# A two-layer trunk on one core: seven products of quarters for eight in layer 0's second FFN product too, three row tiles at the head of both FFNs, and the second half of the tokens completed first

## The chip, the cores and the metric

The kernel runs on one core of a Trainium2 chip. The metric is the device time of one execution in microseconds (us), lower is better. PE is the matrix engine TensorE, DVE is VectorE, ACT is ScalarE, POOL is GpSimd, and SP is the engine whose queue issues nearly all DMAs here.

## The reference

The kernel computes two transformer-like layers in float32 on 512 tokens of width 1024. Layer 0 has a gated-MLP mixer, layer 1 an attention whose keys, values and forget gates are projected once, after layer 0 (the "kv stage"). Both layers end with a SwiGLU FFN of hidden width 2816. Every sublayer is normalised before and after, with shift, scale and gate that come from a conditioning vector `c`:

```
for layer in range(2):
    mod = c_act @ ada_w[layer] + ada_b[layer]
    sh_m, sc_m, g_m, sh_f, sc_f, g_f = split(mod, 6)
    ...
    h = modulate(rms_norm(x, pre_ffn_g[layer]), sh_f, sc_f)
    g, u = split(h @ ffn_w_gu[layer], 2)
    y = (silu(g) * u) @ ffn_w_down[layer]
    x = x + g_f * rms_norm(y, post_ffn_g[layer])
    if layer == 0:
        k, v, dcum = shared_kv(x, c_act @ kv_ada_w + kv_ada_b, ...)
```

## The kernel before, in words

**Products.** Each float32 operand is split into a rounded part "hi" and a remainder "lo" (`load_split`, L112, for loaded weights), and each product is three matmuls: hi by hi, hi by lo, lo by hi. A matmul of 128x512 is the usual piece. Tokens are 4 tiles of 128; the hidden width of the FFN is 22 row tiles of 128. Weights stream from DRAM through a ring of three tiles of 512 KB called `raw` (L110).

**FFN, first product** (`ffn`, L483). For row tile m the gate half and the up half (each 512 KB of `w_gu`, 24 matmuls of 128x512, L504) are formed, then `act` (L506) computes SiLU and the product. The first two row tiles are done in halves of 256 tokens, so that PE can work on tokens 0 to 255 while the hidden state of tokens 256 to 511 is still being normalised, transposed on PE (L277) and split (`prenorm_half`, L268). The lo part of row tile 1's weights is computed on POOL, its hi part on DVE (L525). The normalisation itself is a string of small DVE and ACT steps (`rsqrt1`, L158) that ends in the scaled row `xr` on ACT (L265), on which the transposes wait.

**FFN, second product.** Layer 0 uses `moving` (L284): two column halves, 11 weight pieces each, 3x2 matmuls for each of 4 token tiles, 528 matmuls of 128x512 in all. Layer 1 (`fast`) uses `down` (L362): tokens and columns are halved, the hidden pieces too, and 7 products of quarters (accumulated in X, Z, Y, W and V) replace 8, 462 matmuls (L397 to L399). Its operands are sums of quarters: those of the activations are formed on POOL during the first product (`sums`, L519), those of the weights on DVE (`weight_sums`, L468), which loads `w_down` (two times 512 KB for each pair of row tiles), makes four subtractions of 128x512 and writes four sums to DRAM (`td`), to be loaded again in `down`.

**Background blocks.** The adaLN vectors of later stages come from 512 KB blocks of `ada_w` and `kv_ada_w`: each is loaded to an SBUF tile and reduced against `c` by one DVE instruction (`ada_block`, L181 to L184). They wait in a list `bg`, and `run_bg` emits one or two at given points: 64 of them belong to layer 0's FFN. While a pool is on the stack `bgp` the block is loaded into a tile `rawb` with a single buffer, else into the `raw` ring:

```
raw = bgp[-1].tile([P, 1024], F32, name="rawb", bufs=1) if bgp else raw_tile()
nc.sync.dma_start(raw, src)
nc.vector.tensor_tensor_reduce(raw, raw, c_bc, 1.0, 0.0, mul, add, dst)
```

A `rawb` load can be issued only when the reduce before it has ended, and SP issues its DMAs in the order in which they stand, as DVE executes its instructions.

**What sets the order.** The tile framework's scheduler orders each engine's instructions from the program text, its priorities (`high_priority` in `boundary`) and its own estimates; the order is fixed when the program is built. At the end of layer 0's FFN, `done` (in `boundary`) adds the residual and, for each pair of token tiles, normalises, transposes and splits the hidden state of the kv stage (`evac_h`, L245), whose V and forget-gate products follow for token tiles (0, 1) and then (2, 3) (L859).

Of the kernel before, what the change touches and what calls it, by code (L numbers as in the profile page):

```python
# [68 lines left out]
def tile_yoco_trunk(ctx: ExitStack, tc: tile.TileContext, x, c, cols, ada_t, kv_ada_t,  # L69
# [42 lines left out]
    def load_split(src, width=1024, lo_eng=nc.vector, pool=None, bufs=2, slot=1024, hi_eng=None):  # L112
# [3 lines left out]
        hi = pool.tile([P, slot], F32R, name="whi", tag="whi", bufs=bufs)  # L116
# [4 lines left out]
        lo = pool.tile([P, slot], F32R, name="wlo", tag="wlo", bufs=bufs)  # L121
# [240 lines left out]
    def down(src, td, qa, qb, fp, fw, row, done):  # L362
# [7 lines left out]
        ss = fw.tile([P, 2 * NT], F32, name="ss", bufs=1)  # L370
        X, Z = ([acc.tile([P, 512], F32, name="acc") for _ in range(2)] for _ in range(2))
        Y, W = ([aux.tile([P, 512], F32, name="ps_x", tag=t) for _ in range(2)] for t in ("ps_t", "ps_s"))

# [11 lines left out]
        def parts_q(q, n, held):  # L385

            if held:
                hi, lo = (fp.tile([P, 1024], F32R, name="qh", tag="qb", bufs=NP)[:, :n * H] for _ in range(2))
            else:
                hi, lo = (wp.tile([P, 1024], F32R, name=t, tag=t, bufs=2)[:, :n * H] for t in ("whi", "wlo"))  # L390
            ACT(hi, q, AF.Copy)
            TT(lo, q, f32(hi), sub)
            return lambda i, t: tuple(x[:, i * H + t * P:i * H + t * P + P] for x in (hi, lo))
# [7 lines left out]
        def half_piece(i):  # L401
            r0 = raw_tile()
            nc.sync.dma_start(r0[:, :512], src[0, i, :, 512:])
            return r0[:, :512]

        def held_tile(name, dt=F32):
            return fp.tile([P, 2, 512], dt, name=name, tag="qa", bufs=NP)

        for i in range(NP):
            r0, r1 = raw_tile(), raw_tile()  # L410
            nc.sync.dma_start(r0[:, :512], src[0, i, :, :512])
            nc.sync.dma_start(r0[:, 512:], td[i][:, 0])
            nc.sync.dma_start(r1.rearrange("p (a c) -> p a c", a=2), td[i][:, 1:3])
            a = parts_q(qa[i].rearrange("p q c -> p (q c)"), 4, False)
            for z, (w, bank) in enumerate(((r0[:, :512], X), (r0[:, 512:], Z), (r1[:, :512], Y), (r1[:, 512:], W))):
                w = parts(w)
                for t in range(2):
                    prod(bank[t], a((3, 1, 2, 0)[z], t), w, i == 0, i == NP - 1)
        u2 = held_tile("u2")
        uw = [held_tile("uw") for _ in range(2)]  # L420
        for t in range(2):
            nc.scalar.copy(u2[:, t], X[t])
        for t in range(2):
            TT(u2[:, t], Y[t], u2[:, t], add)
        for t in range(2):
            TT(uw[t][:, 1], Z[t], u2[:, t], add)
            TT(uw[t][:, 0], W[t], u2[:, t], add)
        V = [aux.tile([P, 512], F32, name="ps_x", tag="ps_t") for _ in range(2)]
        held = []
        for i in range(NP):  # L430
            last = i >= NP - TAIL
            r1 = raw_tile()
            nc.sync.dma_start(r1[:, :512], td[i][:, 3])
            nc.sync.dma_start(r1[:, 512:], src[1, i, :, 512:])
            a = parts_q(qb[i].rearrange("p q c -> p (q c)")[:, H:], 3, last)
            b22 = parts(r1[:, 512:], held=last)
            if last:
                held.append([i, a, b22, parts(r1[:, :512])])
                continue
            b21, w3 = parts(half_piece(i)), parts(r1[:, :512])  # L440
# [887 lines left out]
```

## Time and profile before

| | before |
|---|---|
| median of 3 runs | 1385.38 us (1384.28, 1385.38, 1388.41) |
| the profiled execution | 1390.92 us |
| its span, first to last instruction | 1389.2 us |
| PE, DVE, ACT, POOL busy | 96%, 65%, 41%, 20% of the span |
| mean granted clock of PE | 0.989 |
| mean DMA rate | 159 GB/s |

The profiled execution is 5.5 us above the median. Times in the rows count from the start of its span. A row of a timeline gives start, duration, engine, line, operation, tiles and, in brackets, how long the engine had been idle and what released it.

### The profile page before, as it was taken

The page shows a single profiled execution, that of the slowest core. Times are in us where ns is not written, and L with a number is a line of the kernel's source. Part 1 is how long each engine was busy: PE and PEld are TensorE (multiplying, and loading weights), DVE is VectorE, ACT ScalarE, POOL GpSimd, SP SyncE. Part 2 cuts the span into 40 slices and gives each one's busy share as a digit, 9 for nine tenths or more (in the row PEclk, how much of TensorE's full clock was granted, in tenths as well). Part 3 has the DMA queues.
Part 4 walks back from the last instruction along what each step waited for, and adds up shares of the span by engine and source line. Part 5 has one row for each costly group of instructions (what it writes and reads, how often), then busy time and mean ns, then how long its engine had stood idle before and what let it go on. Part 6 is the DMA issues. An engine that isn't in the chain of part 4 may idle for free.

```text
span 1389.2 us, 17713 instructions
## 1 busy us (share of the span) xinstructions
PE 1339.1 (96%) x6463; PEld 1113.0 (80%) x6463; DVE 903.0 (65%) x1569; ACT 572.2 (41%) x983; POOL 278.8 (20%) x228
## 2 busy tenths in 40 slices
PE   6999999998999999899999999999989999999997
PEld 4788888778888888787899777888778888888875
DVE  7888957667545555553554867888676544546777
ACT  5233442354223232123553436778542222224664
POOL 4700000013111111000110535563041211212000
PEclk9999999999999999999999999999999999999999
DMA  8565436833666666673233231011327757565654
GB/s 325 167 218 157 136 110 197 281 110 108 213 201 204 188 193 205 214 249 119 68 104 92 85 96 47 31 32 32 106 77 242 241 177 256 188 213 174 191 152 159
DMA packets 69497, 220.84 MB, mean 159 GB/s; under 512 B 8353, under 2 KB 8609, under 8 KB 69410
## 3 DMA queue, kind: packets, MB, share of 16 engines
q1 hardware_dynamic: 68834, 218.66, 49.4%
q8 instruction: 51, 0.84, 0.3%
q10 hardware_dynamic: 576, 1.05, 0.2%
q14 instruction: 36, 0.29, 0.1%
HBM read 206.03 MB, written 13.65 MB: 158 GB/s over the span
## 4 chain that ended last, share of the span: by engine, by line
PE 57%; DVE 8%; DMA 7%; ACT 2%; issue 2%; POOL 0%; DVEq 0%; SPq 0%; ACTq 0%; POOLq 0%
PE acc L504 32%; PE acc L1012 3%; DMA rawb<-in_ada_t 3%; PE acc L301 3%; PE acc L302 3%; PE acc L300 3%; DMA raw<-in_w_down 2%; DMA raw<-in_ada_t 2%; PE acc L1100 1%; DVE wlo L122 1%; PE ps_z L1053 1%; PE ps_x L277 1%; PE acc L1080 1%; PE ps_s L1065 1%; PE acc L1232 1%
## 5 line engine op out<-in xcount | busy, mean ns | idle before, releaser
L504 PE MATMUL acc<-hT,whi 128*128 128x512 f32 (+1 forms) x1536 | 428.8, 372 | 0.0
L118 ACT ACTIVATE whi<-raw 128x1024 fp32r<-128x1024 f32 (+2 forms) x178 | 185.1, 1041 | 449.1 <-PE acc L504 190.0
L504 PEld LDWEIGHTS acc<-hT,whi 128*128 128x128 f32 x1536 | 273.3, 189 | 49.8
L122 DVE TENSOR_TENSOR wlo<-raw,whi 128x1024 fp32r<-128x1024 f32 (+2 forms) x178 | 218.7, 1230 | 143.3 <-ACT whi L118 141.7
L504 PE MATMUL acc<-hT,wlo 128*128 128x512 f32 (+1 forms) x768 | 267.7, 373 | 0.0
L504 PEld LDWEIGHTS acc<-hT,wlo 128*128 128x128 f32 x768 | 137.3, 190 | 25.0
L184 DVE CUSTOM_DVE_ANT_0 rawb<-rawb,c_bc 128x1024 f32<-128x1024 f32 x62 | 79.0, 1274 | 102.2 <-DMA rawb<-in_ada_t 69.3
L301 PE MATMUL acc<-wlo,hT 128*128 128x512 f32 (+1 forms) x352 | 135.8, 386 | 4.4 <-DVE wlo L122 4.3
L302 PE MATMUL acc<-whi,hT 128*128 128x512 f32 (+1 forms) x352 | 135.4, 385 | 0.0
L300 PE MATMUL acc<-whi,hT 128*128 128x512 f32 (+1 forms) x352 | 135.2, 386 | 0.0
L259 POOL TENSOR_TENSOR hT<-hfull,hT 128x256 fp32r<-128x256 f32 (+1 forms) x43 | 44.0, 1033 | 251.1 <-DVE hT L258 126.1
L301 PEld LDWEIGHTS acc<-wlo,hT 128*128 128x128 f32 x352 | 66.5, 189 | 18.7 <-DVE wlo L122 6.3
L300 PEld LDWEIGHTS acc<-whi,hT 128*128 128x128 f32 x352 | 66.4, 189 | 12.8
L302 PEld LDWEIGHTS acc<-whi,hT 128*128 128x128 f32 x352 | 66.5, 189 | 12.5
L517 POOL TENSOR_TENSOR hid<-sg,hid 128x512 fp32r<-128x512 f32 (+1 forms) x24 | 35.8, 1493 | 198.8 <-ACT hid L516 198.8
L122 POOL TENSOR_TENSOR wlo<-raw,whi 128x1024 fp32r<-128x1024 f32 x20 | 54.9, 2751 | 78.6 <-DVE whi L120 46.9
L301 PE MATMUL acc<-wlo,hid 128*128 128x512 f32 x144 | 56.7, 393 | 3.5 <-DVE wlo L122 3.5
L382 DVE TENSOR_TENSOR hT<-raw,hT 128x512 fp32r<-128x512 f32 x69 | 46.3, 703 | 18.3 <-ACT hT L381 18.2
L300 PE MATMUL acc<-whi,hid 128*128 128x512 f32 x144 | 56.2, 391 | 1.3 <-ACT junk L327 1.1
L184 DVE CUSTOM_DVE_ANT_0 raw<-raw,c_bc 128x1024 f32<-128x1024 f32 x34 | 42.9, 1261 | 22.2 <-DMA raw<-in_ada_t 22.2
L302 PE MATMUL acc<-whi,hid 128*128 128x512 f32 x144 | 56.2, 390 | 0.0
L381 ACT ACTIVATE hT<-raw 128x512 fp32r<-128x512 f32 x69 | 41.7, 627 | 26.1 <-DMA raw<-in_w_down 7.7
(336 smaller groups left out, 2480.9 us busy)
## 6 DMA issues: line engine op xcount, KB each, us to landing
raw<-in_w_gu SPq DMA_DIRECT2D x88, 512.0 KB, 4.4
raw<-in_ada_t SPq DMA_DIRECT2D x50, 512.0 KB, 4.6
rawb<-in_ada_t SPq DMA_DIRECT2D x46, 512.0 KB, 4.2
raw<-in_w_down SPq DMA_DIRECT2D x44, 512.0 KB, 4.3
raw<-in_w_in SPq DMA_DIRECT2D x32, 512.0 KB, 3.7
raw<-in_w_down SPq DMA_DIRECT2D x33, 256.0 KB, 3.0
raw<-in_w_out SPq DMA_DIRECT2D x16, 512.0 KB, 3.7
rawb<-in_kv_ada_t SPq DMA_DIRECT2D x16, 512.0 KB, 3.7
```

The lines of the kernel that those rows point to most:

```text
L118: ACT(hi[:, :width], raw[:, :width], AF.Copy)
L122: lo_eng.tensor_tensor(lo[:, :width], raw[:, :width], f32(hi[:, :width]), sub)
L184: nc.vector.tensor_tensor_reduce(raw, raw, c_bc, 1.0, 0.0, mul, add, dst)
L259: last = lo_eng.tensor_tensor(lo, full, f32(hi), sub)
L300: MM(banks[n], lh, wh, start=kt == 0, stop=False)
L301: MM(banks[n], lh, wl, start=False, stop=False)
L302: MM(banks[n], ll, wh, start=False, stop=kt == kts - 1)
L381: ACT(hi, w, AF.Copy)
L382: TT(lo, w, f32(hi), sub)
L504: MM(o, (hi, hi, lo)[z][:, ks], h[z == 1][kt][:, cs], start=i == 0, stop=i == 3 * KT - 1)
L517: nc.gpsimd.tensor_tensor(hid[1][m][:, cs], sg, f32(hid[0][m][:, cs]), sub)
L1012: pin(MM(box[0], (hi, hi, lo)[z][:, cs], h[z == 1][kt], start=kt + z == 0, stop=kt == KT - 1 and z == 2))
```

## The change

It has four parts.

1. **`down` for both layers.** `ffn` loses its parameter `fast` and the plain path. Layer 0's first product now also holds `weight_sums` and `sums`; its second product is `down`.
2. **Head.** `FIRST = 3` row tiles are done in halves of 256 tokens, and all their weights are split on ACT and DVE, none on POOL. The third tile's parts lie in slots of the pool that later hold `qb`.
3. **`down` in another order.** After the loop that fills X, Z, Y and W, V is completed for all pieces, and token tiles 2 and 3 are finished (`second`) before the last Z and X products, which finish token tiles 0 and 1. Background blocks are emitted in the first loop (`run_bg(1)`) and use `rawb` in the pool `fd`.
4. **kv stage.** The V and forget-gate products take token tiles (2, 3) first.

```diff
-    def down(src, td, qa, qb, fp, fw, row, done):
+    def down(src, td, qa, qb, fp, fd, row, done):
...
         for i in range(NP):
...
+            r0 = halves(src[0, i, :, :512], td[i][:, 0])
+            r1 = halves(td[i][:, 1], td[i][:, 2])
+            a = parts_q(qa[i])
+            run_bg(1)
+            for z, (w, bank) in enumerate(zip(r0 + r1, (X, Z, Y, W))):
                 w = parts(w)
                 for t in range(2):
                     prod(bank[t], a((3, 1, 2, 0)[z], t), w, i == 0, i == NP - 1)
...
-        for i in range(NP):
-            last = i >= NP - TAIL
...
-            for t in range(2):
-                prod(Z[t], a(1, t), b22, False, False)
-            for t in range(2):
-                prod(X[t], a(2, t), b21, False, False)
-            for t in range(2):
-                prod(V[t], a(0, t), w3, i == 0, False)
...
+        for i in range(0, NP, 2):
+            two = range(i, min(i + 2, NP))
+            r, a = halves(*(td[k][:, 3] for k in two)), parts_q(*(qb[k][:, 1:2] for k in two))
+            for k in two:
+                w = parts(r[k - i])
+                for t in range(2):
+                    prod(V[t], a(k - i, t), w, k == 0, k == NP - 1)
         g = row()
...
+        second(0)
+        held = []
+        for i in range(2, NP):
...
+        second(1)
         for t in range(2):
...
-    def ffn(layer, h, row, done, fast=False):
+    def ffn(layer, h, row, done):
...
-                    if fast:
-                        i = m // 2
-                        outs = ((qb[i][:, 3], qa[i][:, 0]) if m % 2 else (qa[i][:, 3], qb[i][:, 0]))
-                        for z, half in enumerate(range(cs.start // H, cs.stop // H)):
-                            TT(outs[half], sg[:, z * H:z * H + H], u[:, z * H:z * H + H], mul)
-                        return
-                    TT(sg, sg, u, mul)
-                    ACT(hid[0][m][:, cs], sg, AF.Copy)
-                    nc.gpsimd.tensor_tensor(hid[1][m][:, cs], sg, f32(hid[0][m][:, cs]), sub)
+                    i = m // 2
+                    outs = ((qb[i][:, 3], qa[i][:, 0]) if m % 2 else (qa[i][:, 3], qb[i][:, 0]))
+                    for z, half in enumerate(range(cs.start // H, cs.stop // H)):
+                        TT(outs[half], sg[:, z * H:z * H + H], u[:, z * H:z * H + H], mul)
...
-                ws = [[load_split(w_gu[layer, m, j], pool=(wp, fw)[m], hi_eng=(None, nc.vector)[m],
-                                  lo_eng=(nc.vector, nc.gpsimd)[m]) for j in range(2)] for m in range(2)]
+                ws = [[load_split(w_gu[layer, m, j], pool=(wp, fw, fp)[m], tag=(None, None, "qb")[m],
+                                  bufs=(2, 2, NF // 2)[m]) for j in range(2)] for m in range(FIRST)]
...
-                for m in range(2, NF):
+                for m in range(FIRST, NF):
...
-                        if m > 2:
+                        if m > FIRST:
                             with behind_norm():
                                 run_bg(1 if layer else 1 + j)
...
-                    if fast and m % 2:
+                    if m % 2:
                         sums(m // 2)
                         weight_sums(w_down[layer], m // 2, td[m // 2])
...
-                moving([w_down[layer, 0, i] for i in range(NF // 2)], NF, 512, lhs, first_half(y0, ss, row))
-                moving([w_down[layer, 1, i] for i in range(NF // 2)], NF, 512, lhs,
-                       lambda n, ps: done(n, ps, y0, ss, row()), tail=6,
-                       tail_load=lambda i, src: load_split_h(src) if i > 1 else cols_of(load_split(src), 512))
+                bgp.append(fd)
+                down(w_down[layer], td, qa, qb, fp, fd, row, done)
+                bgp.pop()
...
-            for grp in ((0, 1), (2, 3)):
+            for grp in ((2, 3), (0, 1)):
```

**PE at the head of layer 0's FFN**, from the last half row before the first transposes of tokens 256 to 511 to the last ones (`xr` is the scaled row of a token tile, `hT` the hidden state, `whi` and `wlo` the parts of a weight tile). Before:

```order
L504 MATMUL acc<-hT,whi 128x256 x16
L277 MATMUL ps_x<-ident,xr 128x128 x4
L504 MATMUL acc<-hT,wlo 128x256 x8
L504 MATMUL acc<-hT,whi 128x256 x16
L504 MATMUL acc<-hT,wlo 128x256 x8
L504 MATMUL acc<-hT,whi 128x256 x9
L277 MATMUL ps_x<-ident,xr 128x128 x12
```

Now:

```order
L531 MATMUL acc<-hT,whi 128x256 x16
L278 MATMUL ps_x<-ident,xr 128x128 x4
L531 MATMUL acc<-hT,wlo 128x256 x8
L531 MATMUL acc<-hT,whi 128x256 x16
L531 MATMUL acc<-hT,wlo 128x256 x8
L531 MATMUL acc<-hT,whi 128x256 x16
L531 MATMUL acc<-hT,wlo 128x256 x8
L531 MATMUL acc<-hT,whi 128x256 x13
L278 MATMUL ps_x<-ident,xr 128x128 x12
```

Between the two groups of transposes stood 41 matmuls of 128x256; now 69 stand there. The same rows stand at the head of layer 1's FFN.

**SP in layer 0's second product** (`rawb` is the single background buffer; `td4` to `td10` hold the stored weight sums; numbers behind a name tell tiles apart). Before, in the first column half:

```order
L183 DMA raw_4564<-in_ada_t 128x1024
L183 DMA rawb_4253<-in_ada_t 128x1024
L114 DMA raw_4591<-in_w_down 128x1024
L183 DMA raw_4597<-in_ada_t 128x1024
L183 DMA rawb_4256<-in_ada_t 128x1024
L114 DMA raw_4624<-in_w_down 128x1024
L183 DMA raw_4630<-in_ada_t 128x1024
L183 DMA rawb_4295<-in_ada_t 128x1024
```

Now, where V is formed:

```order
L184 DMA rawb_4639<-in_ada_t 128x1024
L382 DMA raw_5312<-td4_2619 128x512
L382 DMA raw_5312<-td5_2620 128x512
L382 DMA raw_5341<-td6_2621 128x512
L382 DMA raw_5341<-td7_2622 128x512
L184 DMA rawb_4692<-in_ada_t 128x1024
L184 DMA rawb_4745<-in_ada_t 128x1024
L382 DMA raw_5370<-td8_2623 128x512
L382 DMA raw_5370<-td9_2624 128x512
L382 DMA raw_5399<-td10_2625 128x512
L184 DMA rawb_4798<-in_ada_t 128x1024
```

Two loads of 256 KB now share one tile of the ring, background loads stand between the loads of one tile and the next, and two of them follow each other directly. Of the 64 background loads of this FFN, 50 stand ahead of the last loads of the first loop of `down` and 14 from there to the first loads of the kv weights `w_vf`; before, the last stood in the first column half.

**DVE at the end of layer 0's second product** (L184, now L185, is the reduce of a background block; the CASTs into `hT` make the hi parts of the kv stage's hidden state). Before, the last two reduces:

```order
L184 ISA rawb_4405,A_f1_2608<-rawb_4405,c_bc_75 128x1024
L184 ISA A_f1_2608 128x1
L122 TENSOR_TENSOR wlo_4760<-raw_4756,whi_4758 128x1024
L184 ISA rawb_4408,A_f1_2608<-rawb_4408,c_bc_75 128x1024
L184 ISA A_f1_2608 128x1
L205 TENSOR_TENSOR A_f1_2608<-A_f1_2608,colv_78 128x8
L206 SCALAR_TENSOR_TENSOR A_f1_2608<-A_f1_2608,colv_78 128x8
L122 TENSOR_TENSOR wlo_4805<-raw_4801,whi_4803 128x1024
L331 TENSOR_TENSOR y0_4420<-acc_4431,grow_3191 128x512
```

Now, the last reduce:

```order
L185 ISA rawb_5418,B_f1_2609<-rawb_5418,c_bc_75 128x1024
L185 ISA B_f1_2609 128x1
L165 SCALAR_TENSOR_TENSOR rq_0_5828<-sx2_2611 128x1
L259 CAST hT_5698<-hfull_5730 128x256
L255 TENSOR_SCALAR hfull_5744<-ps_x_5739,A_kv_2603,B_kv_2604 128x256
L168 RECIPROCAL rst2_2610<-rq_1_5829 128x1
L259 CAST hT_5699<-hfull_5734 128x256
L169 TENSOR_TENSOR rq_1_5829<-rst2_2610 128x1
L255 TENSOR_SCALAR hfull_5748<-ps_x_5739,A_kv_2603,B_kv_2604 128x256
```

The last reduce stood ahead of the column half that was still to come; now it stands directly ahead of the first hidden state of the kv stage.

## Rows read from the trace of the kernel before

**Rows 1.** Page, part 1: PE's busy time, share of the span, instructions.
```profile
PE 1339.1 (96%) x6463; PEld 1113.0 (80%) x6463; DVE 903.0 (65%) x1569; ACT 572.2 (41%) x983; POOL 278.8 (20%) x228
```

**Rows 2.** Windows by stage: us, busy (x) of PE, PEld, DVE, ACT, POOL; PEclk, DMA, GB/s.
```profile
330.00:540.00 210.00, 210.00 (x991) 176.66 (x991) 111.41 (x153) 65.66 (x85) 35.74 (x27) 1.00 0.63 193
...
540.00:640.00 100.00, 95.12 (x414) 76.97 (x413) 56.31 (x80) 21.41 (x28) 4.13 (x3) 1.00 0.67 212
...
1037.00:1274.00 237.00, 237.00 (x1106) 199.25 (x1105) 124.51 (x167) 63.21 (x77) 51.27 (x48) 0.99 0.64 209
...
1274.00:1389.00 115.00, 104.43 (x455) 84.70 (x453) 86.56 (x137) 67.06 (x113) 2.24 (x2) 0.98 0.55 172
```

**Rows 3.** PE timeline, layer 0, head of FFN: start, us, instruction, [idle before <-releaser].
```profile
305.05 1.53 PE L277 MATMUL ps_x<-ident,xr 128*128 128x128 f32 x12 [0.31 <-ACT xr L265]
...
317.25 0.66 PE L277 MATMUL ps_x<-ident,xr 128*128 128x128 f32 x4 [1.54 <-ACT xr L265]
...
326.91 2.82 PE L277 MATMUL ps_x<-ident,xr 128*128 128x128 f32 x12 [4.09 <-ACT xr L265]
```

**Rows 4.** PE timeline, layer 1, head of FFN.
```profile
1034.45 2.82 PE L277 MATMUL ps_x<-ident,xr 128*128 128x128 f32 x12 [4.10 <-ACT xr L265]
...
1042.06 1.12 PE L504 MATMUL acc<-hT,wlo 128*128 128x256 f32 x8
1043.02 2.08 PE L504 MATMUL acc<-hT,whi 128*128 128x256 f32 x16
```

**Rows 5.** DVE timeline, layer 0, same head as rows 3.
```profile
320.63 2.35 DVE L164 SCALAR_TENSOR_TENSOR rq<-sx 128x1 f32<-128x1 f32 x1
...
323.45 1.83 DVE L168 TENSOR_TENSOR rq<-rst 128x1 f32<-128x1 f32 x1
325.32 0.16 DVE L169 SCALAR_TENSOR_TENSOR rq<-rq,rq 128x1 f32<-128x1 f32 x1
```

**Rows 6.** POOL timeline, layer 0, same head as rows 3.
```profile
320.19 5.07 POOL L122 TENSOR_TENSOR wlo<-raw,whi 128x1024 fp32r<-128x1024 f32 x2 [5.55 <-DVE whi L120]
```

**Rows 7.** PE timeline, layer 0, second FFN product, to the first kv matmul (L867).
```profile
563.56 0.39 PE L300 MATMUL acc<-whi,hid 128*128 128x512 f32 x1
...
564.92 0.39 PE L300 MATMUL acc<-whi,hid 128*128 128x512 f32 x1
...
577.35 0.50 PE L301 MATMUL acc<-wlo,hid 128*128 128x512 f32 x1 [1.95 <-DVE wlo L122]
...
584.47 0.50 PE L301 MATMUL acc<-wlo,hid 128*128 128x512 f32 x1 [1.39 <-DVE wlo L122]
...
629.75 0.50 PE L300 MATMUL acc<-whi,hid 128*128 128x512 f32 x1 [1.10 <-ACT junk L327]
...
692.57 0.32 PE L867 MATMUL acc<-whi,hT 128*128 128x352 f32 x1
```

**Rows 8.** Chain of waits, layer 0, start of the second product: start, us, what.
```profile
559.58 4.95 DMA rawb<-in_ada_t
564.65 1.22 DVE rawb L184
565.91 3.62 DMA rawb<-in_ada_t
569.67 1.43 DVE rawb L184
```

**Rows 9.** SP timeline: first and last issue of a run of 17 rawb loads.
```profile
530.57 0.33 SPq L183 DMA_DIRECT2D rawb<-in_ada_t  x1
...
621.98 0.33 SPq L183 DMA_DIRECT2D rawb<-in_ada_t  x1
```

**Rows 10.** Page, part 5: three DVE groups; busy, mean ns of one, idle before.
```profile
L122 DVE TENSOR_TENSOR wlo<-raw,whi 128x1024 fp32r<-128x1024 f32 (+2 forms) x178 | 218.7, 1230 | 143.3 <-ACT whi L118 141.7
...
L184 DVE CUSTOM_DVE_ANT_0 rawb<-rawb,c_bc 128x1024 f32<-128x1024 f32 x62 | 79.0, 1274 | 102.2 <-DMA rawb<-in_ada_t 69.3
...
L382 DVE TENSOR_TENSOR hT<-raw,hT 128x512 fp32r<-128x512 f32 x69 | 46.3, 703 | 18.3 <-ACT hT L381 18.2
```

More of the change, by code (lines that the diff above doesn't have):

```diff
@@ L115, in load_split @@
         pool = pool or wp
[L116 removed]
+        hi = pool.tile([P, slot], F32R, name="whi", tag=tag or "whi", bufs=bufs)
         if hi_eng is None:
@@ L422, in down @@
             nc.scalar.copy(u2[:, t], X[t])
+        r, a = halves(b21(0), b21(1)), parts_q(qb[0][:, 3:], qb[1][:, 3:])
+        for i in range(2):
+            w = parts(r[i])
+            for t in range(2):
+                prod(X[t], a(i, t), w, False, False)
         for t in range(2):
             TT(u2[:, t], Y[t], u2[:, t], add)
+        V = [aux.tile([P, 512], F32, name="ps_x", tag="ps_t") for _ in range(2)]
         for t in range(2):
@@ L457, in down @@
             done(n, uw[t][:, 0], uw[t][:, 1], ss, g)
+        r, a = halves(b22(0), b22(1)), parts_q(qb[0][:, 2:3], qb[1][:, 2:3])
+        for i in range(2):
+            w = parts(r[i])
+            for t in range(2):
+                prod(Z[t], a(i, t), w, False, False)
+        second(0)
+        held = []
+        for i in range(2, NP):
+            last = i >= NP - TAIL
+            r, a = halves(b22(i), b21(i)), parts_q(qb[i][:, 2:], held=last)
+            w = [parts(x, last) for x in r]
+            if last:
+                held.append((i, a, w))
+                continue
+            for z, bank in enumerate((Z, X)):
+                for t in range(2):
+                    prod(bank[t], a(z, t), w[z], False, False)
+        second(1)
         for t in range(2):
-            for i, a, b22, w3, b21 in held:
-                prod(Z[t], a(1, t), b22, False, i == NP - 1)
+            for i, a, w in held:
+                prod(Z[t], a(0, t), w[0], False, i == NP - 1)
             TT(u2[:, t], Z[t], u2[:, t], add)
@@ L463, in down @@
             TT(u2[:, t], u2[:, t], g[:, 512:], mul)
-            for i, a, b22, w3, b21 in held:
-                prod(X[t], a(2, t), b21, False, i == NP - 1)
+            for i, a, w in held:
+                prod(X[t], a(1, t), w[1], False, i == NP - 1)
             done(t, X[t], u2[:, t], ss, g)
@@ L552, in ffn, with boundary @@
                             weight_sums(w_down[layer], 0, td[0])
[L553 to L554 removed]
                 bgp.pop()
[L556 to L557 removed]
             with tc.tile_pool(name=f"fd{layer}", bufs=1) as fd:
[L559 to L567 removed]
+                bgp.append(fd)
+                down(w_down[layer], td, qa, qb, fp, fd, row, done)
+                bgp.pop()
+    def boundary(sx, rst, box, a, b, keep=None, raw=1):
         def done(n, ps, y0, ss, row):
             with tc.high_priority():
[L571 removed]
+                residual(n, y0[:, n, :] if raw else y0, ps, ss, row, sx, raw)
                 xrs(n, sx, rst)
[L573 removed]
+                if n % 2 and not box:
                     box.append(new_h())
```

100 lines of the change are left out of this document (42 added, 58 removed).

## The prediction

> **What bounds the kernel now.** I read the page first: PE is busy 96% of the span [rows 1], so fewer matmuls can shorten the run, but only where PE is not waiting. The windows by stage say where that holds. In layer 0's first product PE works 210.00 of 210 us, in layer 1's 237.00 of 237; the 100 us that hold most of layer 0's second product have 95.12 of 100, and layer 1's last 115 us have 104.43 [rows 2]. The PE timelines of the two FFN heads show what is missing there: a wait of 4.09 us in layer 0 and 4.10 us in layer 1 before the second group of transposes, for the scaled row `xr` [rows 3, 4]. In layer 0's second product PE waits three times for more than a microsecond, for a weight split on DVE or an evacuation [rows 7]. The chain of waits tells why: it does not run through PE, but from a background load to its reduce on DVE to the next load [rows 8]. `rawb` has one buffer, so the loads are strung on one thread, and the whole change is judged by whether that thread is shorter than PE's work.
>
> **Matmuls.** Six matmuls take 1.36 us from the first to the second row of [rows 7], 0.2267 us each. Layer 0's second product goes from 528 to 462: 66 x 0.2267 = 15.0 us less PE work. Before, it took 692.57 - 563.56 = 129.0 us where its matmuls alone take 119.7, so 9.3 us were waits and transposes, 4.4 of them the three waits shown. Now 104.7 us of matmuls remain, and about 3 us for 16 transposes (12 take 1.53 [rows 3]) and a short wait.
>
> **Head of layer 0's FFN.** Before, PE stood from 322.8 to 326.9. With three row tiles, 28 more matmuls of 128x256 stand between the two groups of transposes; eight take 0.96 us [rows 4], so PE comes 3.4 us later, at 326.2. And `xr` comes sooner: while POOL split weights for 5.07 us [rows 6], two steps of one column on DVE took 2.35 and 1.83 us [rows 5], where the next such step took 0.16; without POOL there some 3.9 us go. In their place two to four weight splits of 1.23 us [rows 10] come to DVE; with about two of them between the steps `xr` is ready at 325.5. I count the wait as gone (with four splits, 1.7 us of it stay), and with it the slow transposes after it, 2.82 us where 1.53 is usual [rows 3], 1.29 less. The third row tile costs 96 x 0.12 in place of 48 x 0.2267, 0.64 more. Sum -4.7 us: the first product ends at 558.9 in place of 563.56. The wait of 1.54 us before the first transposes stays.
>
> The Trainium skill, page "SBUF — State Buffer", section "Who interferes with whom", says that a DVE instruction with two SBUF inputs contends with a GpSimd instruction that reads SBUF. The long steps beside POOL agree with it, and it speaks against the change in one place, the sums on POOL that layer 0 now gets.
>
> **Layer 0's first product.** It gains what layer 1's has: two loads of `w_down`, four subtractions and three stores for each pair of row tiles, and sums on POOL; it loses the copies into `hid` on ACT and POOL. In layer 1 POOL is busy 51.27 us in this stage and PE still never idles [rows 2], so the sums by themselves cost nothing there. Were DVE held for all of POOL's time, layer 0 would have 111 us of DVE work, 51 of that and 34 of subtractions (48 at 0.70 [rows 10]) in 229 us, still under the span. What is new is that background blocks come on top: about 3.6 blocks, 4 units of `w_gu`, 2 of `w_down` and 2 of stores for each pair of row tiles, 6.1 MB in 21.8 us, 280 GB/s where this stage has 193 and layer 1's has 209 [rows 2]. With 6.05 us for each block PE keeps its pace as long as a block's cycle is below that; I count nothing, and the rival below has the other case.
>
> **The thread of background loads.** By the order of the changed kernel, load 40 of 64 is issued only after reduce 39, which stands on DVE behind the product of row tile 20. That tile ends one tile (10.9 us) before the end of the first product, at 548; with SiLU, product, a split and the reduce (1.23 and 1.27 us [rows 10]) load 40 goes out at about 552. Twenty-five cycles later reduce 64 is done, and the first split of the kv stage's hidden state stands directly behind it on DVE. So the kv stage cannot start before 552 + 25c + 1, where c is one cycle. The hidden pieces' splits and the loads of `td` in V stand between, on DVE and in SP's queue, so PE is held to the same thread on its way.
>
> What c is: in [rows 8] one cycle was 565.91 - 559.58 = 6.33 us, and the next, with a flight of 3.62 and a usual reduce of 1.22, comes to 5.0. Over 17 issues the mean is (621.98 - 530.57) / 16 = 5.71 [rows 9]. These are my bounds, 5.0 and 6.3. In the first loop of `down` DVE does four splits of 0.70, one of 1.23 and one reduce of 1.27 for each piece [rows 10], 5.3 us, and PE 24 matmuls, 5.44 us; there c is PE's pace. For the other 14 I take the middle of the shortest and the mean, a little above because splits stand ahead of the reduces: c = 5.45 on the whole. Then the kv stage starts at 689.2 in place of 692.57 [rows 7]: -3.4 us. PE's own path, 558.9 + 104.7 + 3, would have it at about 667, -25.6. So some 22 us of the gain of head and products are spent waiting for background blocks that layer 0's old second product hid by being longer and by a second ring for part of them.
>
> The Trainium skill, page "DMA: Bandwidth & Descriptors", section "Anatomy of one DMA — SWDGE (gpsimd) path", gives 2.0 us plus bytes over 436 GB/s, 3.2 us for such a load, though for GpSimd's path. By it c would be 4.7 as an estimate, and the sum that of the first rival; the flights of 3.62 and 4.95 us here speak against it.
>
> **Start of the kv stage.** Two weight splits of its products, which were done ahead, now stand behind the evacuation on DVE: 2 x 1.23, +2.5 us. Taking tokens (2, 3) first goes with the order in which they are finished, and costs nothing by itself.
>
> **Layer 1.** Head: -4.10 for the wait. The order has 31 matmuls between those transposes and the row at 1042.06; at 0.12 and with 1.53 for the transposes that row would begin at 1039.7, so 2.4 us more were lost to slow work after the wait [rows 4]. With +0.64 for the third row tile, -5.8. The cover is the same as in layer 0. The tail of the last product: tokens 2 and 3 are finished before the last Z and X products, so their residual leaves DVE sooner; but the last two token tiles are still normalised and stored after the last matmul. Idle time of 10.6 us in this stage [rows 2] is one bound, 0 the other; nearest to 0, -1.0.
>
> **Sum:** -3.4 + 2.5 - 5.8 - 1.0 = -7.7 us. Against the profiled execution of 1390.9 that is 1383.2; this execution stands 5.5 above the median of the runs, so the median should be 1385.4 - 7.7 = 1377.7, rounded to 1378.
>
> **The rivals.**
> *The thread is hidden.* If c falls to 4.6 or less, the kv stage starts with PE at 667 and the sum is -25.6 + 2.5 - 5.8 - 1.0 = -29.9: 1355.5. For it: 256 KB loads leave gaps, and the blocks of V come two in a row. Against it: no cycle shown is that short. By the Trainium skill, page "DMA: Bandwidth & Descriptors", same section, the thread would come close to this case. Chance 0.13.
> *The thread gets longer.* Loads per cycle rise from 2.3 units of 512 KB (212 GB/s over 5.71 us [rows 2, 9]) to about 2.8 (22 units in the first loop, 22 after it and 25 blocks, in 25 cycles), and SP's queue holds the V loads behind two background loads in a row; DVE shares time with POOL. At c = 6.2, near the long cycle of [rows 8], the kv stage starts at 708, +15.4, and the sum is +11.1: 1396.5. It decides from c = 5.92, where the sum passes +4.2. The same mechanism in the first product, with c above 6.05, would first show as PE waits there. Chance 0.21.
> That the change does not do what it says I leave out: the order shows 462 matmuls in both second products and no POOL split in either head.
>
> **How the numbers follow.** The forecast has 0.66, c from 5.0 (1366) to 5.9 (1389), which is its own range. A measurement of this kernel can tell about 0.3%, 4.2 us, from no change; the sum is below -4.2 for c under 5.58, and between the two limits up to 5.92. Of the 0.66 I put 0.46 below and 0.20 between. So faster 0.46 + 0.13 = 0.59, same 0.20, slower 0.21. The range reaches from the first rival, 1356, to the second, 1396.
>
> **What would show it.** Right: no wait near 4 us before the second transposes in either head; PE busy through layer 0's first product; loads of `rawb` some 5.45 us apart from 552 on, with PE waiting behind them in V and at the end; first kv matmul near 689. Wrong: that matmul at 670 or before, or past 700; waits in the first product; or a wait that stays in the heads because the splits on DVE delay `xr` as much as POOL did.

## The result, and the profile after

The change makes the kernel slower: 1405.76 us (median of 4) against 1386.89 (median of 4), a ratio of 1.014 with a 95% interval of 1.0109 to 1.0171. The forecast was 1378, its range ended at 1396. The profiled execution took 1405.30 us, its span 1403.6.

The page of the changed kernel, part 1, and its windows by stage (columns as in [rows 2]):

```profile
PE 1330.5 (95%) x6493; PEld 1104.3 (79%) x6493; DVE 981.1 (70%) x1742; ACT 605.6 (43%) x1066; POOL 280.4 (20%) x244
```

```profile
330.00:540.00 210.00, 205.91 (x993) 173.81 (x992) 131.34 (x197) 49.51 (x60) 43.32 (x42) 0.99 0.80 265
540.00:640.00 100.00, 86.97 (x368) 69.58 (x367) 72.43 (x111) 43.13 (x64) 9.20 (x8) 0.95 0.81 259
640.00:710.00 70.00, 53.86 (x218) 40.60 (x217) 63.40 (x132) 41.16 (x88) 0.00 (x0) 0.94 0.71 230
```

PE's busy time is 8.6 us less than before [rows 1], and yet the run is longer: against [rows 2] PE is idle for 4 us in the window of the first product, where it never was, and for 13 of 100 in the next window, where it was for 5, while DMA carries 265 and 259 GB/s where it carried 193 and 212.

PE's timeline of the changed kernel, layer 0 (the second transposes of the head, then the waits of the two products, and the first kv matmul), and the same transposes in layer 1:

```profile
327.48 1.53 PE L278 MATMUL ps_x<-ident,xr 128*128 128x128 f32 x12 [0.16 <-ACT xr L266]
...
454.86 0.73 PE L531 MATMUL acc<-hT,whi 128*128 128x512 f32 x2 [3.57 <-ACT whi L119]
...
577.19 0.79 PE L415 MATMUL acc<-hT,whi 128*128 128x512 f32 x1 [10.85 <-DVE hT L393]
577.78 0.63 PE L416 MATMUL acc<-hT,wlo 128*128 128x512 f32 x1
...
652.35 1.22 PE L416 MATMUL ps_x<-hT,wlo 128*128 128x512 f32 x2 [3.20 <-DVE wlo L408]
...
709.71 2.82 PE L278 MATMUL ps_x<-ident,xr 128*128 128x128 f32 x12 [6.58 <-ACT xr L266]
713.20 0.66 PE L882 MATMUL acc<-whi,hT 128*128 128x352 f32 x1 [0.67 <-DVE hT L259]
...
1057.92 1.53 PE L278 MATMUL ps_x<-ident,xr 128*128 128x128 f32 x12 [0.16 <-ACT xr L266]
```

The waits of 4.09 and 4.10 us in the heads [rows 3, 4] are 0.16 now. New are a wait in the first product, one of 10.85 us at the seam between layer 0's products, and others to the end. Behind the longest of them the granted clock is 0.51 in the five microseconds from 577, the lower of PE's two levels. The first kv matmul comes at 713.20, not 692.57 [rows 7].

By stage, from PE's timelines, before and after, in us (from the starts of the first and last matmuls of each):

| | before | after | difference | forecast |
|---|---|---|---|---|
| start of the kv stage (first L867, now L882) | 692.57 | 713.20 | +20.6 | -3.4 |
| from there to layer 1's first product | 329.9 | 333.6 | +3.7 | +2.5 |
| layer 1's first product | 249.5 | 243.4 | -6.1 | -5.8 |
| layer 1's second product | 107.4 | 105.4 | -2.0 | -1.0 |

The four add up to the +16.2 us by which the last matmul moved. All but the first are near the forecast. Layer 0's FFN itself began 1.1 us later in the profiled execution (314.77, before 313.64), so its own part of the +20.6 is 19.5.

DVE's timeline of the changed kernel, reduces 5 and 38 to 40, the first split of `down`, and reduce 64:

```profile
358.62 1.22 DVE L185 CUSTOM_DVE_ANT_0 rawb<-rawb,c_bc 128x1024 f32<-128x1024 f32 x1
...
563.76 1.22 DVE L185 CUSTOM_DVE_ANT_0 rawb<-rawb,c_bc 128x1024 f32<-128x1024 f32 x1
...
570.40 1.23 DVE L185 CUSTOM_DVE_ANT_0 rawb<-rawb,c_bc 128x1024 f32<-128x1024 f32 x1 [3.61 <-DMA rawb<-in_ada_t]
...
575.30 1.23 DVE L185 CUSTOM_DVE_ANT_0 rawb<-rawb,c_bc 128x1024 f32<-128x1024 f32 x1 [3.67 <-DMA rawb<-in_ada_t]
576.45 0.08 DVE L185 DVE_READ_ACCUMULATOR2_ANT B_m<- 128x1 f32 x1
576.45 0.69 DVE L393 TENSOR_TENSOR hT<-raw,hT 128x512 fp32r<-128x512 f32 x1
...
711.64 1.23 DVE L185 CUSTOM_DVE_ANT_0 rawb<-rawb,c_bc 128x1024 f32<-128x1024 f32 x1 [1.59 <-DMA rawb<-in_ada_t]
```

The split that PE waits for at the seam stands behind two reduces, and each of these waits for its own load. By SP's timeline, load 40 was issued at 571.7, not 552.

### The profile page after: what moved, and what is told of

It is laid out like the page before. It is cut to its first block, busy times and chain, and to the rows that moved or that the text cites. A ratio compares the mean times of both kernels' runs of the same rounds, so it can differ in the third digit from the quotient of the medians.

```text
span 1403.6 us, 18316 instructions
## 1 busy us (share of the span) xinstructions
PE 1330.5 (95%) x6493; PEld 1104.3 (79%) x6493; DVE 981.1 (70%) x1742; ACT 605.6 (43%) x1066; POOL 280.4 (20%) x244
## 5 line engine op out<-in xcount | busy, mean ns | idle before, releaser
L119 ACT ACTIVATE whi<-raw 128x1024 fp32r<-128x1024 f32 (+2 forms) x164 | 170.0, 1038 | 384.9 <-DMA raw<-in_w_gu 194.7
L123 DVE TENSOR_TENSOR wlo<-raw,whi 128x1024 fp32r<-128x1024 f32 (+2 forms) x164 | 202.5, 1237 | 153.6 <-ACT whi L119 151.4
L185 DVE CUSTOM_DVE_ANT_0 rawb<-rawb,c_bc 128x1024 f32<-128x1024 f32 x72 | 90.7, 1260 | 71.7 <-DMA rawb<-in_ada_t 56.3
L392 ACT ACTIVATE hT<-raw 128x512 fp32r<-128x512 f32 x138 | 84.1, 625 | 62.6 <-DMA raw<-td 38.4
L393 DVE TENSOR_TENSOR hT<-raw,hT 128x512 fp32r<-128x512 f32 x138 | 92.2, 701 | 14.7 <-ACT hT L392 14.5
L547 POOL TENSOR_TENSOR qa<-qb,qa 128x256 f32<-128x256 f32 x22 | 29.9, 1361 | 240.1 <-DVE qa L541 240.1
L415 PE MATMUL acc<-hT,whi 128*128 128x512 f32 x144 | 57.4, 399 | 12.4 <-DVE hT L393 12.4
L416 PE MATMUL acc<-hT,wlo 128*128 128x512 f32 x144 | 57.6, 400 | 2.4 <-DVE wlo L408 2.4
L537 ACT ACTIVATE sg<-acc 128x512 f32<-128x512 f32 (+1 forms) x50 | 26.6, 536 | 77.0 <-PE acc L531 56.1
L414 PE MATMUL acc<-hT,whi 128*128 128x512 f32 x144 | 56.1, 396 | 2.5 <-ACT hT L392 2.3
L123 POOL TENSOR_TENSOR wlo<-raw,whi 128x1024 fp32r<-128x1024 f32 x16 | 44.8, 2800 | 59.8 <-DVE whi L121 36.9
```

The source lines that it names most:

```text
L119: ACT(hi[:, :width], raw[:, :width], AF.Copy)
L123: lo_eng.tensor_tensor(lo[:, :width], raw[:, :width], f32(hi[:, :width]), sub)
L392: ACT(hi, w, AF.Copy)
L393: TT(lo, w, f32(hi), sub)
L414: MM(bank, ah, wh, start=start, stop=False, skip_group_check=True)
L415: MM(bank, ah, wl, start=False, stop=False, skip_group_check=True)
```

## Experiments

Ratios are to the kernel before, timed on the same chip; "kv" is the start of the first kv matmul in the profile, "CHANGED" has 1.014 and kv 713.2. The profiled executions were not all on one chip, and layer 0's FFN begins anywhere from 313.6 to 318.0 us in them, so kv can tell only differences of more than some 4 us. A diff shows the lines that matter; `...` stands for what is left out.

**Two buffers in `down`.** `rawb` in the pool `fd` gets a second buffer.

```diff
-        raw = bgp[-1].tile([P, 1024], F32, name="rawb", bufs=1) if bgp else raw_tile()
+        raw = bgp[-1].tile([P, 1024], F32, name="rawb", bufs=bgb[0]) if bgp else raw_tile()
...
+                bgb[0] = 2
                 down(w_down[layer], td, qa, qb, fp, fd, row, done)
...
```

> The changed kernel with two buffers for rawb in the pool that down uses (one before); the blocks emitted in the first product keep their single buffer, so about the last 13 of 64 can overlap a load with a reduce. Theory T (the single thread of load, reduce, next load holds PE): those 13 cycles fall from 5.7 us towards DVE's pace of 4.5 to 5, the first kv matmul comes at 700 to 706 in place of 713, and the time at 1393 to 1400 us in place of 1405.8. Rival W (the amount of DVE work and of DMA bytes in layer 0's second product holds PE, whatever the buffers): within 3 us of the changed kernel, 1403 to 1408.

Measured: 1.0153 (1.0124 to 1.0182), kv 715.4: rival W. The last reduce on DVE and the first kv matmul on PE, this run:

```profile
682.15 1.22 DVE L186 CUSTOM_DVE_ANT_0 rawb<-rawb,c_bc 128x1024 f32<-128x1024 f32 x1
```

```profile
715.39 0.43 PE L885 MATMUL acc<-whi,hT 128*128 128x352 f32 x1
```

The blocks are done 29 us sooner and the kv stage starts no sooner. In CHANGED the last reduce does end just ahead of the first kv matmul, but the end of the thread alone does not set the start of the kv stage: with it out of the way, longer waits of PE ahead of it (4.53 us at 651, 5.29 at 658, 3.25 at 685) take its place. My theory in this form falls.

**Sixteen blocks later.** A floor on the list keeps the 17 entries of `f1` back; the K and Q projections run them (`n_bg`).

```diff
-            if bg:
+            if len(bg) > hold[0]:
                 bg.popleft()()
...
```

> The changed kernel, with the last 16 background blocks of layer 0's FFN (shift and scale of layer 1's FFN) left in the list and run beside the K and Q projections. T: the thread ends at block 48, near 622, and PE runs the rest of down freely: first kv matmul near 692, and the time 1384 to 1390 us, less if the seam at the start of down shortens too; the K and Q projections give back 0 to 5 us. W: only 16 reduces of 1.26 us and 8 MB leave the stage, and the kv stage starts at 700 or later: 1390 to 1398. If only the lag built up in the first product counts: 1400 or more.

Measured: 1.0077 (1.0061 to 1.0093), kv 692.48. The kv stage starts where T expected it; the time was missed (1401.33 us, T had 1384 to 1390), because from there to layer 1's first product it takes 349.9 us in place of 333.6, 16 where 0 to 5 were expected. PE's timeline of this run, in the projections:

```profile
790.74 0.79 PE L304 MATMUL acc<-wlo,hT 128*128 128x512 f32 x1 [5.51 <-DVE wlo L123]
...
820.90 0.80 PE L304 MATMUL acc<-wlo,hT 128*128 128x512 f32 x1 [3.83 <-DVE wlo L123]
```

Of 20.7 us gained 16 are given back where the blocks went.

**Layer 0 as before.** Layer 0's FFN and the order of the kv stage from the kernel before, layer 1 as changed (`ffn_plain` is the old `ffn`).

```diff
-    ffn(0, hbox[0], lambda: (run_bg(100), g_f0[0])[1], boundary(sx2, rst2, kbox, Ak, Bk, keep, 0))
+    ffn_plain(0, hbox[0], lambda: (run_bg(100), g_f0[0])[1], boundary(sx2, rst2, kbox, Ak, Bk, keep))
...
-            for grp in ((2, 3), (0, 1)):
+            for grp in ((0, 1), (2, 3)):
```

> Layer 0's FFN, its plain second product, its head and the order of the kv stage as before; layer 1 as changed (three row tiles at the head, tokens 2 and 3 completed first). If the gains of layer 1 are its own: head -6, tail -2, so 1378 to 1380 us against 1386.9 before. Rival: the shorter stages of layer 1 only follow from the later start in the changed kernel (buffers freed or loads done meanwhile): 1385 to 1388.

Measured: 0.9937 (0.9922 to 0.9952), 1381.35 us. Layer 1's gains are its own; the loss is layer 0's.

**Loads and reduces apart.** The same 40 of the 64 blocks (those of layer 1's mixer and FFN, for which `skip` is true) in four ways: with both (CHANGED), reduces alone, loads alone, neither, and once with an eighth of the bytes. In `ada_block`, first the reduces alone:

```diff
-        nc.sync.dma_start(raw, src)
-        nc.vector.tensor_tensor_reduce(raw, raw, c_bc, 1.0, 0.0, mul, add, dst)
+        if not skip:
+            nc.sync.dma_start(raw, src)
+        nc.vector.tensor_tensor_reduce(raw, c_bc if skip else raw, c_bc, 1.0, 0.0, mul, add, dst)
```

> The changed kernel, where 40 of the 64 background blocks of layer 0's FFN (those of layer 1's mixer and FFN) are not loaded and their reduces run on the resident vector c, so their DVE work stays, 40 times 1.26 us, and the loads and the thread go; the vectors made from these blocks are thus not those of the reference. T: first kv matmul at 668 to 680, time 1362 to 1375 us. W by DVE work: it stays within 8 us of the changed kernel, 1397 to 1406. W by DMA bytes: as T.

Measured: 0.988 (0.986 to 0.990), kv 677.3. T and "DMA bytes" hold, DVE's work does not. Next the loads alone:

```diff
         nc.sync.dma_start(raw, src)
-        nc.vector.tensor_tensor_reduce(raw, raw, c_bc, 1.0, 0.0, mul, add, dst)
+        if skip:
+            nc.vector.memset(dst, 0.0)
+        else:
+            nc.vector.tensor_tensor_reduce(raw, raw, c_bc, 1.0, 0.0, mul, add, dst)
```

> The changed kernel, where the same 40 blocks as in the run without loads are loaded into rawb but not reduced, so that their bytes and their places in SP's queue stay and 50 us of DVE work go, and with them the reduces that stand ahead of weight splits; the vectors made from these blocks are not those of the reference. Theory O (what costs is DVE executing in order: a reduce that waits for its load holds the splits behind it): first kv matmul at 675 to 685, ratio to the kernel before 0.987 to 0.994. Rival B (bytes and in-order loads on SP): first kv matmul at 695 or later, ratio 1.000 or more.

Measured: 1.0057 (1.0037 to 1.0077), kv 702.8: rival B. Then neither:

```diff
+        if skip:
+            nc.vector.memset(dst, 0.0)
+            return
```

> The changed kernel, where the 40 blocks are neither loaded nor reduced, which leaves the vectors made from them other than the reference's: what seven products and the new head bring when only the 24 blocks needed by the kv stage run beside them. With loads alone the kv stage began at 703, with reduces alone at 677, with both at 713. If the two costs add: first kv matmul at 666 to 672, ratio 0.978 to 0.984. If the reduces cost nothing by themselves and only hold splits when their loads are late: 675 to 678, ratio 0.986 to 0.989.

Measured: 0.9871 (0.9853 to 0.9890), kv 678.9: the second expectation in the ratio, a microsecond beyond it in kv. PE's first kv matmul with neither, with reduces alone and with loads alone, three runs:

```profile
678.93 0.43 PE L885 MATMUL acc<-whi,hT 128*128 128x352 f32 x1 [0.19 <-DVE hT L262]
```

```profile
677.26 0.43 PE L883 MATMUL acc<-whi,hT 128*128 128x352 f32 x1 [0.20 <-DVE hT L260]
```

```profile
702.84 0.43 PE L885 MATMUL acc<-whi,hT 128*128 128x352 f32 x1 [0.20 <-DVE hT L262]
```

Fifty microseconds of reduces cost nothing without loads, loads alone cost 24, and both 34 (22 and 36, when each is counted from the start of layer 0's FFN in its own execution). So a reduce cost PE time only where its load was there to be late. That it does so by holding the splits behind it on DVE is seen at the seam above; for the rest of these 10 to 13 us it is argued. What the loads do by themselves is seen on ACT, which makes the hi parts of `down`'s weights: between the first product and the kv stage its idle time that ended with a load of `td` was 36.5 us in CHANGED, 35.9 with loads alone, 10.7 with reduces alone and 3.3 with neither. In the kernel before, the waits that [rows 7] shows in layer 0's second product are 4.4 us in all, so there the same blocks can't have cost anything near 36.

Then an eighth of the bytes:

```diff
-        nc.sync.dma_start(raw, src)
-        nc.vector.tensor_tensor_reduce(raw, raw, c_bc, 1.0, 0.0, mul, add, dst)
+        w = 128 if skip else 1024
+        nc.sync.dma_start(raw[:, :w], src[:, :w])
+        nc.vector.tensor_tensor_reduce(raw, c_bc if skip else raw, c_bc, 1.0, 0.0, mul, add, dst)
```

> The changed kernel, where the same 40 blocks are loaded only in their first 128 of 1024 columns (64 KB in place of 512 KB) and reduced over the full width against resident data: the same number of loads in SP's order, the same single buffer and waits between load and reduce, the same DVE work, an eighth of the bytes; the vectors made from these blocks are not those of the reference. If the bytes cost (B): as without these loads, first kv matmul at 676 to 684, ratio 0.986 to 0.992. If the number of loads and their waits in the queue cost: 695 or later, ratio 1.000 or more. The flight of a load is shorter too, so a value between the two leaves both.

Measured: 0.9995 (0.9978 to 1.0011), kv 692.8, between the two. In its windows DMA carries 192 GB/s from 564 to 640, close to the 186 of the run with neither:

```profile
564.00:640.00 76.00, 68.27 (x286) 53.67 (x284) 68.25 (x108) 40.36 (x65) 4.84 (x4) 0.96 0.64 192
```

Of the 36 us between CHANGED and reduces alone 20 go with the bytes (and with the shorter flights, 2.6 us in place of 4.4), 16 stay with the number of loads and their waits (21 and 14, counted from the start of layer 0's FFN). ACT's idle time ahead of loads of `td` is 19.4 us here, between the others too.

**Two halves in flight.** Each block in two halves through two half-sized buffers.

```diff
...
+        for z, d in enumerate((dst, part)):
+            raw = bgp[-1].tile([P, 512], F32, name="rawb", bufs=2)
+            cs = slice(z * 512, z * 512 + 512)
+            nc.sync.dma_start(raw, src[:, cs])
+            nc.vector.tensor_tensor_reduce(raw, raw, c_bc[:, cs], 1.0, 0.0, mul, add, d)
+        TT(dst, dst, part, add)
...
```

> The changed kernel, where each background block is loaded and reduced in two halves of 256 KB through two buffers of half the size: the same bytes, the same memory, a little more DVE work (two reduces of about 0.7 and an add for one of 1.26), but two loads in flight. By its order some 53 blocks, not 38, now stand on DVE ahead of the first split of layer 0's second product. Theory T (the serial load, reduce, load of one buffer is what costs): the seam wait of 10.85 us falls below 3, the first kv matmul comes at 675 to 690 and the ratio to the kernel before is 0.985 to 0.998. Rival B (too many bytes and transfers at once: 300 GB/s in the first product makes w_gu late): waits of PE for w_gu in the first product of more than 5 us in all, and a ratio of 1.005 or more.

Measured: 1.0126 (1.0101 to 1.0151), kv 710.0. PE's timeline of this run:

```profile
460.60 1.22 PE L540 MATMUL acc<-hT,whi 128*128 128x512 f32 x2 [8.85 <-ACT whi L119]
...
586.23 0.79 PE L424 MATMUL acc<-hT,whi 128*128 128x512 f32 x1 [10.49 <-DVE hT L402]
```

The first product takes 10 us more, the second 12.6 less: rival B.

**Reduces behind the seam.** Two blocks for each row tile in place of three, and in `down` behind the piece's splits.

```diff
-                                run_bg(1 if layer else 1 + j)
+                                run_bg(1)
```

> The changed kernel with two background blocks, not three, for each row tile of layer 0's first product, and two for each piece of the first loop of down, emitted behind that piece's splits: by its order no reduce stands within 8 DVE instructions ahead of the first split of down, 34 blocks are done ahead of it and 30 come after. O: the seam's wait of 10.85 us and the slow matmuls after it go, the first kv matmul comes at 698 to 706, ratio 1.003 to 1.009. T (the length of the thread is conserved): 30 blocks at 5.7 us after 566 end at 737 or so, PE waits for them at the end instead, first kv matmul at 715 or later, ratio 1.012 or more.

Measured: 1.008 (1.006 to 1.0101), kv 708.7: the ratio is in O's range, kv lies between O's and T's. The seam's wait and the wait at the end on PE:

```profile
569.24 0.50 PE L415 MATMUL acc<-hT,whi 128*128 128x512 f32 x1 [3.24 <-DVE hT L393]
```

```profile
706.25 2.82 PE L278 MATMUL ps_x<-ident,xr 128*128 128x128 f32 x12 [6.14 <-ACT xr L266]
```

The seam gives 7.6 us, kv only 4.5: part of the wait moves on. With the 16 blocks of `f1` deferred as well, through a small buffer of their own in a pool beside the projections:

```diff
...
+                raw = bgp[-1].tile([P, 512], F32, name="rawb", bufs=1)
...
+    hold[0] = 17
     ffn(0, hbox[0], lambda: (run_bg(100), g_f0[0])[1], boundary(sx2, rst2, kbox, Ak, Bk, keep, 0))
...
+        bgp.append(bgt.__enter__())
...
```

> As the run before, with the 16 blocks of layer 1's FFN left to the K and Q projections, there in halves through a small buffer of their own instead of the ring of raw. If both costs are what they seem, 14 blocks remain after the seam, PE waits little in layer 0's second product, the first kv matmul comes at 672 to 684, the projections give back 3 to 10 us of that, and the ratio is 0.988 to 0.998. If K and Q give back 16 us as with the ring: 1.000 to 1.004.

Measured: 1.0089 (1.0064 to 1.0113), kv 689.0; the projections take back 19 us, own buffer or not. The forecast was missed in both halves, and the ratio is also above the one expected if 16 us were given back.

**POOL's queue.** The blocks of both FFNs are issued from POOL.

```diff
-        nc.sync.dma_start(raw, src)
+        (nc.gpsimd if bgp else nc.sync).dma_start(raw, src)
```

> The changed kernel with the background blocks of both FFNs issued from POOL's queue instead of SP's, so that a block waiting for its buffer holds no weight load behind it; bytes, buffers and DVE work as they are. If the place in SP's queue is what the loads cost (theory Q): first kv matmul at 685 to 700, ratio 0.992 to 1.004. If it is the bytes and the DMA engines' time (B): first kv matmul at 708 or later, ratio 1.010 or more.

Measured: 1.0537 (1.0514 to 1.0559), kv 773.8. First and last reduce of this run on DVE:

```profile
337.99 1.21 DVE L185 CUSTOM_DVE_ANT_0 rawb<-rawb,c_bc 128x1024 f32<-128x1024 f32 x1
...
747.76 1.22 DVE L185 CUSTOM_DVE_ANT_0 rawb<-rawb,c_bc 128x1024 f32<-128x1024 f32 x1 [0.92 <-DMA rawb<-in_ada_t]
```

A cycle is now (747.76 - 337.99) / 63 = 6.50 us, longer than CHANGED's 5.96, and kv goes 61 us later, in B's range, which was open upward, but far beyond what B gives a reason for. One cause of the longer cycle stands in the timelines, a reduce of this run on DVE and the next issue on POOL:

```profile
606.88 1.23 DVE L185 CUSTOM_DVE_ANT_0 rawb<-rawb,c_bc 128x1024 f32<-128x1024 f32 x1 [3.71 <-DMA rawb<-in_ada_t]
...
608.53 0.58 POOL L184 DMA_DIRECT2D rawb<-in_ada_t  x1 [2.93 <-DVE g_m L185]
```

The next load goes out 0.42 us after the reduce's end, and 0.04 after it on SP (medians of this run and of CHANGED). In the first product, now 300 us long, PE waits most for lo parts of weights from DVE (24.7 us in 17 waits), where the reduces stand between the splits. The queue theory finds no support here, but since the cycle grew, the run doesn't decide it.

**The heads alone.** CHANGED with two row tiles and POOL's splits:

```diff
-            FIRST = 3
+            FIRST = 2
...
-                ws = [[load_split(w_gu[layer, m, j], pool=(wp, fw, fp)[m], tag=(None, None, "qb")[m],
-                                  bufs=(2, 2, NF // 2)[m]) for j in range(2)] for m in range(FIRST)]
+                ws = [[load_split(w_gu[layer, m, j], pool=(wp, fw)[m], hi_eng=(None, nc.vector)[m],
+                                  lo_eng=(nc.vector, nc.gpsimd)[m]) for j in range(2)] for m in range(FIRST)]
```

> The changed kernel with two row tiles at the head of both FFNs and POOL splitting one tile's weights, as before: the rest of the change alone. If layer 0 is held by background loads, only layer 1's part of the head is lost: 5 to 7 us over the changed kernel, ratio 1.018 to 1.019. If both heads count in full: 10 to 11 us, ratio 1.021 to 1.022.

Measured: 1.0188 (1.0159 to 1.0216), 0.0048 or 6.7 us above CHANGED. With the intervals of both ratios this difference is uncertain by about 6 us either way, so the ratios decide nothing. PE's timeline of this run, in layer 0:

```profile
462.16 1.22 PE L531 MATMUL acc<-hT,whi 128*128 128x512 f32 x2 [7.19 <-ACT whi L119]
...
718.47 0.64 PE L882 MATMUL acc<-whi,hT 128*128 128x352 f32 x1
```

The kv stage starts 5.3 us later than in CHANGED, and layer 1's first product takes 249.3 us in place of 243.4. That speaks for both heads counting in full, background loads or not. But these are single executions, and the kernel before was itself 4.7 us slower beside this run than beside CHANGED (1391.64 against 1386.89), so which of the two expectations holds stays open.

Now the run with layer 0 as before, with the third row tile at its head too, its weights in slots that `hid` fills later:

```diff
-                hid = [[fp.tile([P, S], F32R, name=f"hid{q}_{m}") for m in range(NF)] for q in range(2)]
+                    t = fp.tile([P, 2, S], F32R, name="hid", tag="hid", bufs=NF)
...
+                ws = [[load_split(w_gu[layer, m, j], pool=(wp, fw, fp)[m], tag=(None, None, "hid")[m],
+                                  bufs=(2, 2, NF)[m]) for j in range(2)] for m in range(FIRST)]
```

> As e5 (layer 0's second product and kv order as before, layer 1 as changed), with three row tiles at the head of layer 0 as well, none of their weights split on POOL. If the term of the prediction holds, layer 0's first product ends 4.7 us sooner and the ratio goes from 0.9937 (e5) to 0.990. Rival: the background loads set the pace of layer 0's FFN before too, and the gain at its head is waited away in the second product: 0.9925 to 0.9945.

Measured: 0.9903 (0.9883 to 0.9923), 1377.9 us: first product 244.9 us long in place of 249.7, kv 686.7. The term of the prediction holds, and this version beats both kernels. The same with the half blocks of the diff above:

> As e8, with the background blocks in two halves through two buffers of half the size as in e7. If the single buffer cost anything in layer 0's FFN as it was before, the waits of 1.95 and 1.39 us in its second product go and the ratio is 0.986 to 0.989; if not, it equals e8 within 0.002.

Measured: 0.9933 (0.9912 to 0.9954): a little slower than without halves, as expected in neither case. And with the blocks on POOL's queue, by the diff above:

> The version with layer 0's plain second product, three row tiles at both heads and layer 1 as changed (ratio 0.990), with the background blocks of both FFNs issued from POOL's queue. If SP's order costs something there too: 0.985 to 0.989. If not, or if the copies into hid on POOL are held up by the issues: 0.990 or more.

Measured: 0.9982 (0.9967 to 0.9998): slower too.

## Why the prediction was wrong

**Heads: right.** -4.7 us in layer 0 was -4.8 where layer 0 is otherwise as before; in CHANGED the wait of 4.09 us is gone, but what that brought at the kv stage stays open. Layer 1's -5.8 was -6.1. DVE's timeline of the changed kernel shows the step as argued, three splits among the small steps (one of them below) and the steps short again (the long ones are in [rows 5]):

```profile
324.49 0.16 DVE L168 RECIPROCAL rst<-rq 128x1 f32<-128x1 f32 x1
324.57 1.21 DVE L123 TENSOR_TENSOR wlo<-raw,whi 128x1024 fp32r<-128x1024 f32 x1
325.69 0.15 DVE L169 TENSOR_TENSOR rq<-rst 128x1 f32<-128x1 f32 x1
```

**Layer 1's tail and the kv stage: right** within 1.2 us. PE's waits for weight splits behind the start of the kv stage are there (2.19 us at 722.79 and 1.66 at 736.74), and before it had none.

**Layer 0's first product: wrong.** The step that failed is "With 6.05 us for each block PE keeps its pace as long as a block's cycle is below that; I count nothing". From reduce 5 (358.62) to reduce 38 (563.76) a cycle took 6.22 us. PE hardly waited there, 4.1 us at 455 and little else, but load 40 went out at 571.7 in place of 552, and the first part of this debt of 20 us was collected at the seam, where two reduces stand ahead of the first split. Some 7 us of the 20 come from the product itself, which ended at 566 and not at 558.9. The price was in reach: 280 GB/s stood in the text, 193 and 209 in the rows, and of the two cycles of [rows 8] one was 6.33 us, above the 6.05; I counted nothing all the same. The sign that I gave for it, waits of PE in the first product, was too weak: 4.1 us of 20.

**The cycle: half right.** The 24 cycles after reduce 40 took (711.64 - 575.30) / 24 = 5.68 us each, not 5.45; 25 times 0.23 are 5.7 us. With the debt of 19.7 that makes 25.4, and the miss at the kv stage was 24.0: the same sum with these two numbers gives 571.7 + 25 x 5.68 + 1 = 714.7 where 713.2 came. The rival "the thread gets longer" had 708 and came nearest, and its clause on the first product is what happened; but its long cycle of 6.2 us stood ahead of load 40, not behind it, and the measured time lies outside its 1396.5 as well. That the sum comes out so near does not make the thread the cause, as the run with two buffers shows. The first rival's 4.6 us was never reached: the flight alone of a load was 4.4 us in the median behind load 40, and the shortest cycle there was 4.8.

**The mechanism: too narrow.** I took the single buffer, whose last reduce the kv stage must wait for, as the whole cause. With two buffers the last reduce came at 682 and the kv stage at 715; with two halves in flight the time moved from one product to the other. What the runs show is that the 40 blocks' loads, beside weights and stored sums that are already 32 MB more (252.6 MB against 220.8), make loads of `td` late (ACT's 36 us against 3), and that at the seam late reduces hold the split behind them. How much of it is bytes and how much the waits in SP's queue stays open: the run with small loads leaves 16 of 36 us to the waits, but its flights are shorter as well.

**The matmuls: right and not enough.** With reduces alone the second product took 113.2 us where the matmuls are 104.7 and I had 107.7; even so the ratio is 0.988 (0.986 to 0.990), hardly below the 0.9903 (0.9883 to 0.9923) of the version that leaves layer 0's second product as it was and does all of its loads.

## What to carry to other kernels

Here a product with fewer matmuls that streams more bytes did not pay beside the other streams of its stage: price such a product with the transfer times of a stage that is already as full, not of the one that it replaces. A background list that is run in the gaps is a debt; before a stage is shortened, count its blocks times their cycle against the new length, and look at what stands behind them on in-order engines at each seam. Moving such work to another stage has its own price there: 16 of 21 us came back.

## What was unexpected of the hardware

Beside POOL's sums, DVE's subtractions of 128x512 took 1.22 us in place of 0.69. DVE and POOL of the changed kernel:

```profile
559.55 1.22 DVE L500 TENSOR_TENSOR t<-raw 128x512 f32<-128x512 f32 x1
560.69 1.23 DVE L501 TENSOR_TENSOR t<-raw,t 128x512 f32<-128x512 f32 x1
561.96 0.69 DVE L502 TENSOR_TENSOR t<-raw,t 128x512 f32<-128x512 f32 x1
```

```profile
558.59 1.63 POOL L547 TENSOR_TENSOR qa<-qa 128x256 f32<-128x256 f32 x1
560.30 1.07 POOL L547 TENSOR_TENSOR qb<-qb,qa 128x256 f32<-128x256 f32 x1
```

The third one, after POOL's end, is short again. The Trainium skill, page "SBUF — State Buffer", section "Who interferes with whom", has this contention of two-input DVE instructions with GpSimd's reads, and the rows agree. The prediction named these sums on POOL and found room for them; it counted the contention itself only in the head.

Most of what POOL's queue cost the cycle (6.50 us, not 5.96) does not stand in the transfer's own time. In layer 0's FFN the median from issue to landing of a 512 KB load of `ada_t` into `rawb` was 4.4 us on either queue, and of `kv_ada_t` 4.8 on POOL's and 4.2 on SP's; the wait from the reduce's end to the next issue grew from 0.04 to 0.42 us in the median.
